# Merge gates in a stage of their own: twelve projection tiles as six Strassen pairs behind pa, attention left with q and k

## The chip, the cores and the metric

The kernel runs on one core of one Trainium2 chip. The metric is the time on the device in microseconds (us), the median of several runs. TensorE (PE) multiplies matrices, VectorE (DVE) and ScalarE (ACT) work elementwise, GpSimd (POOL) issues some of the DMAs and does a little elementwise work, SyncE (SP) issues the other DMAs.

## The reference

One layer of a hybrid encoder on 512 tokens of width 1024, in float32. It is given x, the weights and the gains:

```python
h = rms_norm(x, mix_norm_pre)
proj = h @ w_in                      # 1024 x 7696
xa, ga, q, k, v, f_logit, g_a, g_b = split(proj)
hr = rg_lru(causal_dwconv(xa), ...)  # recurrent branch, width 1280
y_a = gelu(ga) * hr
y_b = forgetting_attention(q, k, v, f_logit + b_forget)   # 16 heads of 64, causal
merged = (sigmoid(g_a + b_merge[0]) * (y_a @ w_proj_a)
          + sigmoid(g_b + b_merge[1]) * (y_b @ w_proj_b))
x = x + rms_norm(merged @ w_out, mix_norm_post)
h = rms_norm(x, ffn_norm_pre)
gate, val = split(causal_dwconv(h @ w_up))                # 1024 x 6144
x = x + rms_norm((gelu(gate) * val) @ w_down, ffn_norm_post)
```

In forgetting_attention the score of query i and key j is q·k/8 + cum[i] - cum[j], with cum the running sum of log_sigmoid(f). The change concerns g_a and g_b, each 1024 columns of w_in, and when they are computed.

## The kernel before

Each float32 operand is split into a high and a low part in a format that PE takes at full speed, and each product is made of three matmuls: high x high, high x low, low x high. `Split` does this for a weight tile: a load of 512 KB on SP's queue, the high part as a cast on ACT (`wh_...`, L172), the low part as a subtraction on DVE (`wl_...`, L175). A weight tile of w_in has 128 columns; `project` multiplies it with h (`hh`, `hl`, 1024 x 512 tokens) in 8 steps of three matmuls of 512 columns (L222 to L224), 24 in all. `order` lists the weight tiles in the order of their use, and `unit` fetches two ahead, so that list sets the order of the loads.

The stages follow one another on PE: xa and the recurrent gates, v (83 us), ga (136), pa (y_a @ w_proj_a, 190 to 248 us), attention with q, k and the gate tiles ma (to 426), then the tiles mb and pb (y_b @ w_proj_b), wo (517), up (562), dn (801).

The forget gate (`forget`, L626) is computed inside pa, after tile 4: 16 small matmuls, then a long chain of 16 x 512 operations on DVE (log-sigmoid, running sum), then four writes of cum to DRAM (`cnd`). A head's bias tile `B` is read back from there by a broadcast DMA, and two accumulating DMAs add the causal mask; both are issued by POOL (`prep_alloc`, L689). There are two such tiles per period.

Attention has eight periods of two heads. On PE a period is `ma`, `av` (probabilities x v of the heads before), scores, `q`, `k`, `pt` (transposes of the probabilities of this period's heads, which PE's next `av` wants). DVE adds the bias to the scores and takes the row's minimum (L726), ACT takes the exponential (L731), DVE divides by the sum (`normalise`, L738 and L741), then PE transposes in halves (L753), and ACT and DVE split the result (L763, L764). A gate tile's tanh is on ACT (L676), and ma is multiplied into `pa` on DVE (L802). The tiles mb0 to mb2 fill the end of attention, mb3 to mb7 stand between the tiles of pb.

The up stage (L927 to L930) already uses Strassen's form: a class `Pair` takes two weight tiles and computes both with seven products of half the size instead of eight. Each product is 12 matmuls of 256 columns (4 steps, three matmuls each). It needs sums of weight quarters (DVE, `sums`), their high and low parts, sums of quarters of h, and adds of the results. At two pairs (`TURNS`) eight small transposes stand before product 5. The low half of a plain quarter is made by ACT, with the sign turned, and a POOL-issued accumulating DMA (`ml`, L877).

Elsewhere a scheduler decides the place of an instruction within an engine from the order of the code and its waits; under `manual_schedule` the written order holds.

Of the kernel before, what the change touches and what calls it, by code (L numbers as in the profile page):

```python
# [8 lines left out]
F32 = mybir.dt.float32  # L9
# [7 lines left out]
P = 128  # L17
# [9 lines left out]
H = 16  # L27
# [36 lines left out]
def kernel(  # L64
# [120 lines left out]

    order = [(f"xa{t}", *cols(w_in, B_XA + t)) for t in range(TR)]
# [8 lines left out]
    for e in range(KD):  # L195
        if e >= 3:
            order.append((f"mb{e}", *cols(w_in, B_MB + e)))
        order.append((f"pb{e}", *cols(w_pb, e)))
# [110 lines left out]
    def v_out(c, pv):  # L309
        for t in range(NT):  # L310
            pvv = pv[t].rearrange("p (q j d) -> p q j d", q=4, j=2)
            for q in range(4):
                p = 4 * c + q
                vh = vt[p][:, t, 0:4:3, :]
                act.copy(vh, pvv[:, q])
                dve.tensor_tensor(out=vt[p][:, t, 1:3, :], in0=pvv[:, q], in1=vh.bitcast(F32), op=ALU.subtract)

    with ExitStack() as rg:
# [303 lines left out]
        papool = mstk.enter_context(tc.tile_pool(name="pa", bufs=1, reuse_waits="tile"))  # L622
        pa = papool.tile([P, KD, S], F32, name="pa")
        cnd = ctx.enter_context(tc.tile_pool(name="cnd", bufs=1, space=bass.MemoryType.DRAM)).tile([H, PO[NT]], F32, name="cnd")

        def forget():  # L626
            def tl(name, n=H, dt=F32):
                return tpool.tile([P, S], dt, tag="tt", name=f"f_{name}")[0:n]

            fr = tl("fr", P)[:, : KD * H].rearrange("p (k e) -> p k e", k=KD)  # L630
            nc.sync.dma_start(fr, w_f)
            fw = tl("fw", P, F32R)[:, : KD * 48].rearrange("p (k e) -> p k e", k=KD)
# [7 lines left out]
            z = tl("z")  # L640
            act.copy(z, pf[32:48])
            dve.scalar_tensor_tensor(out=z, in0=pf[0:H], scalar=cpt[0:H, C_BF : C_BF + 1], in1=z, op0=ALU.add, op1=ALU.add)
            with tc.issue_after(last_act[0].ins):
                l1p = log1p_exp_neg(z, tl)
            dve.tensor_scalar(out=z, in0=z, scalar1=0.0, scalar2=None, op0=ALU.min)
            dve.scalar_tensor_tensor(out=z, in0=l1p, scalar=-2.0, in1=z, op0=ALU.mult, op1=ALU.add)
            ones = tl("ones")
            pool.memset(ones, 1.0)
            cum = tl("cum")
            dve.tensor_tensor_scan(out=cum, data0=ones, data1=z, initial=0.0, op0=ALU.mult, op1=ALU.add)  # L650
            dve.tensor_scalar(out=cum, in0=cum, scalar1=-8.0, scalar2=None, op0=ALU.mult)
            for b in range(NT):
                nc.sync.dma_start(cnd[:, PO[b] : PO[b + 1]], cum[:, : PO[b + 1] - PO[b]])

        pps = {}
        for e, half in PA_ORDER:
            if half == 0:
                pps[e] = bank(f"pa{e}")
            wh, wl = unit(f"pa{e}_{half}")
# [18 lines left out]

    with ExitStack() as at:
# [88 lines left out]
        def av(p, pts):  # L768
# [14 lines left out]
            yb[p] = vpools[p == 0 or p > 4].tile([P, 2, S], F32R, tag="vy", name=f"yb{p}")  # L783
# [3 lines left out]
        prev = None  # L787
        for p in range(KD):
            bias = prep_alloc(p)
            pq, pk = bank(f"q{p}"), bank(f"k{p}")  # L790
            project(pq, unit(f"q{p}"), hh, hl)
            if prev is not None:
                normalise(prev)
            project(pk, unit(f"k{p}"), hh, hl)
            q = halves(pq, f"q{p}")
            if p == 0:
                apool.tile([P, 64], F32, name="offset_k", bufs=1)
            k = halves(pk, f"k{p}")
# [4 lines left out]
            if prev is not None:  # L803
                av(p - 1, pts)
            prev = scores(p, q, k, bias)
        tgs = [gate_tile(0, "mb")]
        normalise(prev)
        tgs.append(gate_tile(1, "mb"))
        pts = pt(KD - 1, prev)
        tgs.append(gate_tile(2, "mb"))  # L810
# [10 lines left out]
    for e in range(KD):  # L821
        if e >= 3:
            tgs.append(gate_tile(e, "mb"))
# [26 lines left out]
    KH, SH = KD // 2, S // 2  # L850
    TURNS = (NU + 2, NU + 7)

    def sub(out, a, b):
        dve.tensor_tensor(out=out, in0=a, in1=b, op=ALU.subtract)  # L854

    A, B = slice(0, 512), slice(512, 1024)
    X, Y = slice(0, SH), slice(SH, S)

    def quarter(a, b, s):
# [651 lines left out]
```

## The time and the profile before

| | us |
|---|---|
| median of 3 runs (lowest, highest) | 927.65 (926.85, 929.72) |
| the profiled execution | 925.8 |
| its span in the profile | 924.0 |
| PE busy | 913.7 (99%) |
| PE weight loads busy (beside PE) | 797.6 (86%) |
| DVE busy | 685.0 (74%) |
| ACT busy | 565.7 (61%) |
| POOL busy | 223.0 (24%) |

The span goes from the first to the last instruction. PE's granted clock is full throughout. Busy shares are averages over stages: in pa DMA is nearly full and DVE half empty, in the up stage DVE is nearly full. PE is the engine that nearly never waits, so the questions to the trace are what its matmuls take and what could make it wait.

### The profile page before, as it was taken

What the parts mean: (1) busy time and instruction counts of PE and PEld (TensorE: products, weight loads), DVE (VectorE), ACT (ScalarE), POOL (GpSimd) and SP (SyncE); (2) the same over time, 40 slices, a digit from 0 to 9 for tenths busy, and PEclk for the clock granted to TensorE, in tenths of its full rate; (3) what the DMA queues carried; (4) which work ended last, traced back from release to release, by engine and by line L of the source; (5) the groups of instructions that cost most, each with busy time, mean ns of one, the idle gap of its engine ahead of it and who ended that gap; (6) DMA issues with size and microseconds to landing.
All of it is one profiled execution on the core that took longest, in us unless ns stands there. A gap on an engine that the chain in (4) does not pass through costs nothing.

```text
span 924.0 us, 15014 instructions
## 1 busy us (share of the span) xinstructions
PE 913.7 (99%) x5598; PEld 797.6 (86%) x5598; DVE 685.0 (74%) x1127; ACT 565.7 (61%) x981; POOL 223.0 (24%) x235
## 2 busy tenths in 40 slices
PE   8999999999999999999999999999999999999997
PEld 7988888887888888888888889999999999988885
DVE  5966369532857777777544588999899999889897
ACT  7555495333345666666333376698778887667664
POOL 4134345444243232220111000022232323100000
PEclk9999999999999999999999999999999999999999
DMA  7667589989686656653232764188888888799764
GB/s 278 236 210 209 162 203 257 278 215 258 164 229 153 165 149 153 153 151 80 72 111 91 273 184 159 38 227 223 213 231 206 239 204 203 225 347 335 250 212 146
DMA packets 76218, 182.29 MB, mean 197 GB/s; under 512 B 7281, under 2 KB 35745, under 8 KB 75762
## 3 DMA queue, kind: packets, MB, share of 16 engines
q1 hardware_dynamic: 44912, 122.87, 39.7%
q0 software_dynamic: 30944, 57.94, 30.4%
q8 instruction: 44, 0.72, 0.3%
q10 hardware_dynamic: 290, 0.53, 0.1%
q14 instruction: 28, 0.23, 0.1%
HBM read 148.59 MB, written 33.64 MB: 197 GB/s over the span
## 4 chain that ended last, share of the span: by engine, by line
PE 96%; DVE 2%; ACT 1%; DMA 1%; issue 0%; SPq 0%; DVEq 0%; ACTq 0%
PE up L927 7%; PE up L930 7%; PE up L928 7%; PE dn L1234 4%; PE dn L1233 4%; PE dn L1232 4%; PE ga L223 2%; PE ga L222 2%; PE pa L224 2%; PE pa L222 2%; PE pa L223 2%; PE ga L224 2%; PE ma L222 2%; PE q L222 2%; PE wo L846 2%; PE mb L222 2%
## 5 line engine op out<-in xcount | busy, mean ns | idle before, releaser
L1085 DVE SCALAR_TENSOR_TENSOR u<-up,cpt,u 128x511 f32<-128x511 f32 x96 | 71.3, 746 | 2.6 <-ACT u L1079 0.9
L877 POOL DMA_DIRECT2D ml<-raw_up x41 | 35.1, 856 | 144.3 <-ACT mh L886 75.7
L1234 PE MATMUL dn<-wh_dn,al 128*128 128x512 f32 x168 | 65.6, 391 | 0.1
L1232 PE MATMUL dn<-wh_dn,ah 128*128 128x512 f32 x168 | 65.4, 389 | 0.0
L1233 PE MATMUL dn<-wl_dn,ah 128*128 128x512 f32 x168 | 65.4, 389 | 0.0
L927 PE MATMUL up<-sh,th 128*128 128x256 f32 x252 | 61.2, 279 | 0.7 <-ACT x L934 0.6
L928 PE MATMUL up<-sl,th 128*128 128x256 f32 x252 | 60.8, 277 | 0.0
L175 DVE TENSOR_TENSOR wl_dn<-raw_dn,wh_dn 128x1024 fp32r<-128x1024 f32 x42 | 51.5, 1227 | 8.7 <-ACT wh_dn L172 8.7
L172 ACT CAST wh_dn<-raw_dn 128x1024 fp32r<-128x1024 f32 x42 | 44.1, 1050 | 16.3 <-issue 6.0
L854 DVE TENSOR_TENSOR tl<-t,th 128x1024 fp32r<-128x1024 f32 x42 | 51.2, 1218 | 1.3 <-ACT th L908 1.3
L927 PEld LDWEIGHTS up<-sh,th 128*128 128x128 f32 x252 | 47.4, 188 | 1.2 <-ACT x L934 0.8
L928 PEld LDWEIGHTS up<-sl,th 128*128 128x128 f32 x252 | 47.4, 188 | 0.0
L696 POOL DMA_DIRECT2D B<-maskf x32 | 39.4, 1635 | 28.2 <-DMA B<-cnd 24.9
L908 ACT CAST th<-t 128x1024 fp32r<-128x1024 f32 x42 | 44.0, 1048 | 3.0 <-PE up L223 0.8
L1093 POOL TENSOR_TENSOR yf<-u,u 128x512 f32<-128x512 f32 x20 | 25.9, 1296 | 79.8 <-issue 66.8
L1079 ACT ACTIVATE u<-up,cpt 128x512 f32<-128x512 f32 x48 | 36.9, 775 | 12.3 <-POOL yf L1093 8.0
L927 PE MATMUL up<-h2h,mh 128*128 128x256 f32 x168 | 40.5, 277 | 0.0
L928 PE MATMUL up<-h2l,mh 128*128 128x256 f32 x168 | 40.5, 277 | 0.0
L930 PE MATMUL up<-sh,tl 128*128 128x256 f32 x252 | 39.1, 277 | 0.0
L1234 PEld LDWEIGHTS dn<-wh_dn,al 128*128 128x128 f32 x168 | 31.5, 188 | 7.4 <-DVE al L854 0.8
L934 ACT COPY x<-up 128x256 f32<-128x256 f32 x63 | 23.1, 367 | 23.7 <-PE up L930 23.6
L175 DVE TENSOR_TENSOR wl_pa<-raw_pa,wh_pa 128x640 fp32r<-128x640 f32 x16 | 13.1, 820 | 32.7 <-ACT wh_pa L172 32.7
(655 smaller groups left out, 3174.8 us busy)
## 6 DMA issues: line engine op xcount, KB each, us to landing
raw_up<-in_w_up_dram SPq DMA_DIRECT2D x48, 512.0 KB, 5.4
td<-in_w_down_dram POOLq DMA_DIRECT2D x36, 512.0 KB, 7.9
raw_dn<-td SPq DMA_DIRECT2D x24, 512.0 KB, 5.0
B<-cnd POOLq DMA_DIRECT2D x16, 640.0 KB, 5.0
ml<-raw_up POOLq DMA_DIRECT2D x20, 512.0 KB, 5.7
raw_dn<-in_w_down_dram SPq DMA_DIRECT2D x18, 512.0 KB, 4.3
raw_wo<-in_w_out_dram SPq DMA_DIRECT2D x16, 512.0 KB, 3.8
td<-td POOLq DMA_DIRECT2D x12, 512.0 KB, 10.7
```

Source lines behind the costliest of these rows:

```text
L172: act.copy(self.wh, self.raw)
L175: engine.tensor_tensor(out=self.wl, in0=self.raw, in1=self.wh.bitcast(F32), op=ALU.subtract)
L222: pe.matmul(dst, ah, bh, start=first, stop=False)
L854: dve.tensor_tensor(out=out, in0=a, in1=b, op=ALU.subtract)
L908: act.copy(self.th[i], self.t[i])
L927: pe.matmul(dst, wh[:, k], ah[:, k], start=first and k == 0, stop=False, skip_group_check=True)
L928: pe.matmul(dst, wh[:, k], al[:, k], start=False, stop=False, skip_group_check=True)
L930: pe.matmul(dst, wl[:, k], ah[:, k], start=False, stop=k == KH - 1, skip_group_check=True)
L1085: dve.scalar_tensor_tensor(out=c[:, s:], in0=ps[:, : S - s], scalar=col(C_CFW + 3 * e + j), in1=c[:, s:], op0=ALU.mult, op1=ALU.add)
L1232: pe.matmul(dst[t], ah[:, k, tok], wh[:, k], start=first, stop=False, skip_group_check=True)
L1233: pe.matmul(dst[t], ah[:, k, tok], wl[:, k], start=False, stop=False, skip_group_check=True)
L1234: pe.matmul(dst[t], al[:, k, tok], wh[:, k], start=False, stop=last, skip_group_check=True)
```

## The change

Six pairs (ma e, mb e), e = 2 to 7 (`M0` is 2), are computed by `Pair` in a stage of their own behind pa. ma0 and ma1 stay plain and stand at its start; mb0 and mb1 stay plain and stand at the end of attention. `Pair` is made general (a `Stage` holds its pools and operands) and moves up in the file. The gates mb2 to mb7 are written to DRAM (`mbd`) and read back during pb. The forget gate is computed before pa, between it and the end of ga. `h_sums` computes the sums of quarters of h, in the memory that later holds half of pa's results. The attention loop has the order av, k, normalise, pt, q, scores. `hh` and `hl` stay until mb1, and one buffer of the value pool moves to a pool of its own (`vy2`).

```diff
-    for p in range(KD):
-        order.append((f"q{p}", *cols(w_in, B_Q + p)))
-        order.append((f"k{p}", *cols(w_in, B_K + p)))
-        order.append((f"ma{p}", *cols(w_in, B_MA + p)))
-    order += [(f"mb{e}", *cols(w_in, B_MB + e)) for e in range(3)]
...
+    order += [(f"ma{e}", *cols(w_in, B_MA + e)) for e in range(M0)]
+    order += [proj("q", 0), proj("k", 0), proj("q", 1)]
+    for p in range(1, KD):
+        order.append(proj("k", p))
+        if p + 1 < KD:
+            order.append(proj("q", p + 1))
+    order += [(f"mb{e}", *cols(w_in, B_MB + e)) for e in range(M0)]
+    order += [(f"pb{e}", *cols(w_pb, e)) for e in range(KD)]
...
+        with tc.tile_pool(name="forget", bufs=1, reuse_waits="tile") as fpool:
+            forget(fpool)
...
+        def h_sums(i, sh=sh, sl=sl):
+            c1, c2 = (slice(P * (i + d), P * (i + 1 + d)) for d in (0, 2))
+            f = pa[:, KH:].rearrange("p a (k c) -> p a k c", k=KH)
+            f11, f12, f21, f22 = (f[:, a] for a in range(4))
+            for dst, k, c in ((f21, 0, c2), (f22, KH, c2), (f11, 0, c1), (f12, KH, c1)):
+                dve.tensor_tensor(out=dst, in0=hh[:, k : k + KH, c].bitcast(F32), in1=hl[:, k : k + KH, c].bitcast(F32),
+                                  op=ALU.add)
...
+            for n, src in enumerate((f22, f11, f21, f12)):
+                act.copy(sh[n][:, :, c1], src)
+                dve.tensor_tensor(out=sl[n][:, :, c1], in0=src, in1=sh[n][:, :, c1].bitcast(F32), op=ALU.subtract)
...
-            if (e, half) == (4, 1):
-                forget()
...
+            if (e, half) in ((2, 0), (1, 1)):
+                h_sums(half)
...
+        m_pair = lambda p: Pair(mstg, p, (w_in[B_MA + p], w_in[B_MB + p]))
+        gate_tile(0, "ma", 1)
+        mp = {M0: m_pair(M0)}
+        gate_tile(1, "ma", 0)
...
+        def m_out(b, which):
+            tg = gate_act(b.c if which == "mb" else b.a, b.j, which)
+            if which == "mb":
+                nc.sync.dma_start(mbd[b.j], tg)
+
+        def m_period(j):
+            p, b, n1, n2 = mp[j], mp.get(j - 1), mp[j + 1], mp[j + 2]
+            if b:
+                p.p5()
+                b.add(b.c[:, Y], b.a[:, Y], 1)
+                b.add(b.c[:, X], b.c[:, X], 0)
+            n1.plain(1)
+            if b:
+                m_out(b, "mb")
+                p.keep(1, p.c[:, X])
+                n1.sums(0)
+            p.product(6, p.a[:, Y])
...
+                b.product(4, b.a[:, Y])
+                m_out(b, "ma")
...
+            p.product(3, p.c[:, X])
+            n2.plain(0)
+            n1.p12()
...
+            m_load(j)
+            p.product(7, p.a[:, Y])
...
+        prev = scores(0, qs[0], ks[0], bias)
         for p in range(KD):
-            bias = prep_alloc(p)
-            pq, pk = bank(f"q{p}"), bank(f"k{p}")
-            project(pq, unit(f"q{p}"), hh, hl)
-            if prev is not None:
-                normalise(prev)
-            project(pk, unit(f"k{p}"), hh, hl)
...
-                pts = pt(p - 1, prev)
-            tg = gate_tile(p, "ma")
-            dve.scalar_tensor_tensor(out=pa[:, p], in0=tg, scalar=1.0, in1=pa[:, p], op0=ALU.add, op1=ALU.mult)
-            if prev is not None:
+            if p:
                 av(p - 1, pts)
-            prev = scores(p, q, k, bias)
-        tgs = [gate_tile(0, "mb")]
+            if p + 1 < KD:
+                bias = prep_alloc(p + 1)
+                ks[p + 1] = projected("k", p + 1)
+            else:
+                tgs.append(gate_tile(0, "mb"))
+            normalise(prev)
+            pts = pt(p, prev)
+            if p + 2 < KD:
+                qs[p + 2] = projected("q", p + 2)
+            if p + 1 < KD:
+                prev = scores(p + 1, qs[p + 1], ks[p + 1], bias)
...
     for e in range(KD):
-        if e >= 3:
-            tgs.append(gate_tile(e, "mb"))
+        if e + 1 >= M0 and e + 1 < KD:
+            tgs.append(tgps[-1].tile([P, S], F32, tag="tg", name=f"tg_mb{e + 1}"))
+            nc.sync.dma_start(tgs[-1], mbd[e + 1])
         pb = bank(f"pb{e}")
```

Two places show how the order on DVE moves. The first is pa. Before, DVE has there only the low parts of pa's weights (`wl_pa`), and from tile 6 on the chain of the forget gate (`f_...`):

```order
L175 TENSOR_TENSOR wl_pa5_0_2142<-raw_pa5_0_2140,wh_pa5_0_2141 128x640
L175 TENSOR_TENSOR wl_pa5_1_2165<-raw_pa5_1_2163,wh_pa5_1_2164 128x640
L175 TENSOR_TENSOR wl_pa6_0_2245<-raw_pa6_0_2243,wh_pa6_0_2244 128x640
L175 TENSOR_TENSOR wl_pa6_1_2268<-raw_pa6_1_2266,wh_pa6_1_2267 128x640
L642 SCALAR_TENSOR_TENSOR f_z_2210<-f_2193,cpt_82,f_z_2210 16x512
L268 SCALAR_TENSOR_TENSOR f_y_2213<-f_z_2210 16x512
L645 TENSOR_SCALAR f_z_2210<-f_z_2210 16x512
L271 TENSOR_SCALAR f_d_2216<-f_y_2213 16x512
L272 RECIPROCAL f_d_2216<-f_d_2216 16x512
```

After, in the same place of pa, the sums of h (`pa<-hh,hl` and `pa<-pa`, 128 x 512) and their low parts (`msl`) stand between the low parts of the weights:

```order
L175 TENSOR_TENSOR wl_pa5_0_2245<-raw_pa5_0_2243,wh_pa5_0_2244 128x640
L784 TENSOR_TENSOR pa_2005<-hh_117,hl_118 128x512 x4
L786 TENSOR_TENSOR pa_2005<-pa_2005 128x512
L175 TENSOR_TENSOR wl_pa5_1_2268<-raw_pa5_1_2266,wh_pa5_1_2267 128x640
L787 TENSOR_TENSOR pa_2005<-pa_2005 128x512
L792 TENSOR_TENSOR msl0_2013<-pa_2005,msh0_2012 128x4x128
L788 TENSOR_TENSOR pa_2005<-pa_2005 128x512
L792 TENSOR_TENSOR msl2_2017<-pa_2005,msh2_2016 128x4x128
L789 TENSOR_TENSOR pa_2005<-pa_2005 128x512
L792 TENSOR_TENSOR msl1_2015<-pa_2005,msh1_2014 128x4x128
```

The forget chain has gone ahead of these rows, and the low part of pa5_1 stands behind the first five sums.

The second place is an attention period. `P6`, `P7` are the probabilities of heads 6 and 7, `s6`, `s7` their scores, `B` the bias tiles, `y2` the sum of the two halves of `av`'s result of the heads before. Before, DVE adds y ahead of the bias steps:

```order
L782 TENSOR_TENSOR y2_3287<-av4_3289,ytmp2_3288 64x512
L782 TENSOR_TENSOR y2_3287<-av5_3300,ytmp2_3288 64x512
L726 ISA P6_3344,mx6_3345<-s6c_3316,B6_3099 128x512
L726 ISA mx6_3345 128x1
L726 ISA P7_3355,mx7_3356<-s7c_3319,B7_3103 128x512
L726 ISA mx7_3356 128x1
L785 TENSOR_TENSOR yb2_3311<-y2_3287,yb2_3311 128x512
L726 ISA P6_3344,mx6_3345<-s6b_3315,B6_3099 128x256
L726 ISA mx6_3345 128x1
L726 ISA P7_3355,mx7_3356<-s7b_3318,B7_3103 128x256
```

After, y is added between the steps of the second head's normalising:

```order
L981 RECIPROCAL sm6_4158<-sm6_4158 128x4
L984 TENSOR_SCALAR P6_4156<-P6_4156,sm6_4158 128x512
L984 TENSOR_SCALAR P6_4156<-P6_4156,sm6_4158 128x384
L984 TENSOR_SCALAR P6_4156<-P6_4156,sm6_4158 128x128
L984 TENSOR_SCALAR P6_4156<-P6_4156,sm6_4158 128x256
L981 RECIPROCAL sm7_4169<-sm7_4169 128x4
L984 TENSOR_SCALAR P7_4167<-P7_4167,sm7_4169 128x512
L1025 TENSOR_TENSOR y2_4178<-av4_4180,ytmp2_4179 64x512
L1025 TENSOR_TENSOR y2_4178<-av5_4191,ytmp2_4179 64x512
L984 TENSOR_SCALAR P7_4167<-P7_4167,sm7_4169 128x384
L984 TENSOR_SCALAR P7_4167<-P7_4167,sm7_4169 128x128
```

The adds of y have moved behind the bias steps and the first head's normalising, and three of the second head's four steps stand behind them.

## Rows read from the trace of the kernel before

**Rows 1.** The page, part 1: engine, busy us (share of the span), instructions.
```profile
PE 913.7 (99%) x5598; PEld 797.6 (86%) x5598; DVE 685.0 (74%) x1127; ACT 565.7 (61%) x981; POOL 223.0 (24%) x235
```

**Rows 2.** Waits of PE: waiting line, releaser, us in all, times, longest.
```profile
PE xa L421 <- POOL ident masks.py:199: 1.5, 1, 1.5
```

**Rows 3.** Windows: pa, one attention period, the Strassen part of the up stage.
```profile
core 0: us, PE busy (x) PEld busy (x) DVE busy (x) ACT busy (x) POOL busy (x), PEclk, DMA share, GB/s
190.00:248.00 58.00, 58.00 (x257) 46.94 (x256) 27.59 (x34) 19.76 (x28) 23.62 (x27) 1.00 0.96 215
324.67:347.36 22.69, 22.69 (x156) 19.06 (x152) 16.65 (x44) 13.83 (x35) 6.93 (x7) 1.00 0.56 149
597.30:800.60 203.30, 202.59 (x1771) 201.66 (x1770) 186.64 (x274) 163.00 (x252) 58.02 (x59) 1.00 0.85 219
```

**Rows 4.** Timeline of PE at three seams: start, us, engine, line, operation.
```profile
135.82 0.39 PE L222 MATMUL ga<-hh,wh_ga 128*128 128x512 f32 x1
...
190.22 0.39 PE L222 MATMUL pa<-yh,wh_pa 128*128 128x512 f32 x1
...
248.33 0.39 PE L222 MATMUL q<-hh,wh_q 128*128 128x512 f32 x1
```

**Rows 5.** Timeline of PE, 256-column matmuls of the up stage.
```profile
562.29 0.28 PE L222 MATMUL up<-h2h,wh_up 128*128 128x256 f32 x1
...
573.48 0.28 PE L224 MATMUL up<-h2h,wl_up 128*128 128x256 f32 x1
...
642.10 0.63 PE L930 MATMUL up<-sh,tl 128*128 128x256 f32 x4
...
643.51 0.64 PE L930 MATMUL up<-h2h,tl 128*128 128x256 f32 x4
...
669.51 0.46 PE L946 MATMUL up<-ident 64*128 64x64 f32 x8
...
672.30 0.62 PE L930 MATMUL up<-sh,tl 128*128 128x256 f32 x4
...
673.66 0.62 PE L930 MATMUL up<-h2h,tl 128*128 128x256 f32 x4
```

**Rows 6.** DMA issues: tile, queue, count, KB each, us to landing.
```profile
ml<-raw_up POOLq DMA_DIRECT2D x20, 512.0 KB, 5.7
...
B<-maskf POOLq DMA_DIRECT2D x32, 128.0 KB, 5.2
```

**Rows 7.** Timeline of DVE in pa (columns as in rows 4).
```profile
191.75 0.69 DVE L592 TENSOR_TENSOR gelu<-gelu,ix 128x512 f32<-128x512 f32 x1
...
228.73 0.74 DVE L642 SCALAR_TENSOR_TENSOR f_z<-f,cpt,f_z 16x512 f32<-16x512 f32 x1 [2.90 <-ACT f_z L641]
...
250.16 0.41 DVE L651 TENSOR_SCALAR f_cum<-f_cum 16x512 f32<-16x512 f32 x1
```

**Rows 8.** Timeline of PE, one attention period.
```profile
307.56 0.39 PE L777 MATMUL av<-PTh,v 128*128 128x512 f32 x1
...
310.13 0.49 PE L717 MATMUL s4c<-h_k,h_q 64*128 64x512 f32 x1
...
312.20 0.50 PE L222 MATMUL q<-hh,wh_q 128*128 128x512 f32 x1
...
323.29 0.71 PE L753 MATMUL pt<-ident,P 64*128 64x64 f32 x16
```

**Rows 9.** Timeline of DVE, the same period.
```profile
310.36 1.40 DVE L782 TENSOR_TENSOR y<-av,ytmp 64x512 f32<-64x512 f32 x2
311.80 0.69 DVE L726 CUSTOM_DVE_ANT_0 P<-s4c,B 128x512 f32<-128x512 f32 x1
...
317.81 1.27 DVE L741 TENSOR_SCALAR P<-P,sm 128x512 f32<-128x512 f32 x4
```

**Rows 10.** Timeline of POOL, the same period.
```profile
315.39 1.25 POOL L693 DMA_DIRECT2D B<-cnd  x2 [13.29 <-DVE mx L726]
...
323.24 2.42 POOL L696 DMA_DIRECT2D B<-maskf  x2 [0.49 <-DMA B<-cnd]
```

More of the change, by code (lines that the diff above doesn't have):

```diff
@@ L316, in v_out, with sub, quarter, __init__ @@
                 dve.tensor_tensor(out=vt[p][:, t, 1:3, :], in0=pvv[:, q], in1=vh.bitcast(F32), op=ALU.subtract)
+    KH, SH = KD // 2, S // 2
+    def sub(out, a, b):
+        dve.tensor_tensor(out=out, in0=a, in1=b, op=ALU.subtract)
+    A, B = slice(0, 512), slice(512, 1024)
+    X, Y = slice(0, SH), slice(SH, S)
+    def quarter(a, b, s):
+        return tuple(x[:, s].rearrange("p (k e) -> p k e", k=KH) for x in (a, b))
+    class Stage:
+        def __init__(self, name, turns=()):
+            self.name, self.turns = name, turns
@@ new lines @@
+        with tc.tile_pool(name="forget", bufs=1, reuse_waits="tile") as fpool:
+            forget(fpool)
+        papool = mstk.enter_context(tc.tile_pool(name="pa", bufs=1, reuse_waits="tile"))
+        pa = papool.tile([P, KD, S], F32, name="pa")
+        mstg = Stage("m")
+        sums = ExitStack()
+        spool = sums.enter_context(tc.tile_pool(name="msums", bufs=1, reuse_waits="tile"))
+        sh, sl = {}, {}
+        for pad, parts in ((0, (3,)), (192, (0, 1, 2))):
+            if pad:
+                spool.tile([P, pad // 4], F32, name="offset_ms")
+            for i in parts:
+                sh[i] = spool.tile([P, KH, SH], F32R, name=f"msh{i}")
+                sl[i] = spool.tile([P, KH, SH], F32R, name=f"msl{i}")
@@ L658 @@
                 pps[e] = bank(f"pa{e}")
-            wh, wl = unit(f"pa{e}_{half}")
+            wh, wl = unit(f"pa{e}_{half}", min(2, where["ma0"] - where[f"pa{e}_{half}"]))
             for i in range(5):
@@ new lines, with gate_act @@
+    mbd = [ctx.enter_context(tc.tile_pool(name=f"mbd{e}", bufs=1, space=bass.MemoryType.DRAM)).tile([P, S], F32, name=f"mbd{e}")
+           for e in range(KD)]
+    tgps = []
+    def gate_act(pg, e, which):
+        c = 0 if which == "ma" else KD
+        tg = tgps[-1].tile([P, S], F32, tag="tg", name=f"tg_{which}{e}")
+        act.activation(out=tg, in_=pg, func=AF.Tanh, scale=0.5, bias=hb[:, c + e : c + e + 1])
+        if which == "ma":
+            dve.scalar_tensor_tensor(out=pa[:, e], in0=tg, scalar=1.0, in1=pa[:, e], op0=ALU.add, op1=ALU.mult)
+        return tg
@@ L679 @@
+    sums.close()
+    vpools.append(mstk.enter_context(tc.tile_pool(name="vy2", bufs=1, reuse_waits="tile")))
+    tgps.append(mstk.enter_context(tc.tile_pool(name="tg", bufs=3, reuse_waits="tile")))
     with ExitStack() as at:
@@ L806, with projected @@
-        tgs = [gate_tile(0, "mb")]
-        normalise(prev)
+        def projected(n, p):
+            if (n, p) == ("q", 0):
+                ps = pq
+            else:
+                ps = bank(f"{n}{p}")
+                project(ps, unit(f"{n}{p}"), hh, hl)
+            return halves(ps, f"{n}{p}")
+        qs = {0: projected("q", 0)}
+        apool.tile([P, 64], F32, name="offset_k", bufs=1)
+        ks = {0: projected("k", 0)}
+        bias = prep_alloc(0)
+        qs[1] = projected("q", 1)
```

304 lines of the change are left out of this document (175 added, 129 removed).

## The prediction

> **What bounds the kernel now.** I read the page's first part before all else: TensorE (PE) is busy 913.7 of 924.0 us, VectorE (DVE) 685.0, ScalarE (ACT) 565.7, GpSimd (POOL) 223.0 [rows 1]. Then the waits of PE: the longest is 1.5 us, and it lies at the start [rows 2]. So PE never waits for long; a change is worth what it takes out of PE's stream of matmuls, less the new waits that it makes there. Hence the table of windows, stage by stage: it shows how much of DVE, ACT and DMA lies under PE where the change adds work and where it takes cover away [rows 3]. In pa (190 to 248) DVE is busy 27.59 of 58.00 us; one attention period takes 22.69 us of PE, beside 16.65 of DVE. Last, PE's timeline gives the price of one matmul in each width, and DVE's and POOL's the chain of one attention period.
>
> **What is removed.** Twelve tiles (ma and mb of e = 2 to 7) leave attention and pb, each 24 matmuls of 512 columns. From the first of ga at 135.82 to the first of pa at 190.22 stand 10 tiles, 240 matmuls, without a gap [rows 4]: 54.40 / 240 = 0.2267 us each. 288 x 0.2267 = 65.3 us.
>
> **What is added.** Six pairs, each of 7 products of 12 matmuls of 256 columns: 42 products. The kernel already has such products in its up stage, and they run at two speeds: the groups at 642.10 and 643.51 stand one product apart, 1.41 us; those at 672.30 and 673.66 stand 1.36 apart [rows 5]. The speed changes at the little transposes (669.51), not at a wait, and the first 256-column matmuls after a 512-column stage (562.29 to 573.48, 95 spacings) took 11.19 / 95 = 0.1178 us each, 1.41 a product, until the next transposes [rows 5]. So 42 x 1.36 = 57.1 or 42 x 1.41 = 59.2. The new stage also follows 512-column work, which speaks for the slow speed, but which of the two a stage inherits I can't read from one entry; the whole up stage, 147 products in 203.30 us with its waits [rows 3], stands at 1.38. I take 1.385, between both: 58.2. Exchange: -7.1 us (ends -8.2 and -6.1).
>
> At full speed 256 columns cost half of 512 (1.36 / 12 = 0.1133 against 0.2267) [rows 4, 5], so the width costs nothing there; at the slow speed it costs 4%. The Trainium skill, Perfetto Trace Analysis, section Optimizing Tensor Performance, says that larger matmuls are more efficient than smaller ones, which speaks against this form; by it alone all 42 products run slow and the exchange would be -6.1, the time 923.7. The trace bears it out in one part of the up stage and not in the other.
>
> **Does the new stage feed PE?** One pair per 9.5 to 9.9 us needs on DVE two sum steps, two low parts and the adds (about as in up, where DVE is busy 186.64 of 203.30 us for 21 pairs and with conv and GeLU beside them [rows 3]); here conv and GeLU are absent. PE ran in up nearly without a gap, so I add nothing per pair. The seam is the start: the first pair's low half comes by an accumulating transfer of 5.7 us [rows 6]. Its ACT part can start when pa ends (248.3 [rows 4]); two plain tiles, ma0 and ma1, cover 2 x 5.44 = 10.9 us; by my walk through the order the transfer lands some 2.6 us before the first product wants it. I allow 0.3 to 0.4 us for small bubbles (0 to 3).
>
> **pa gets DVE work.** The half-sums of h are 24 more operations on 128 x 512 (the multiply of that size at 191.75 took 0.69 us [rows 7]) and 8 casts on ACT: DVE goes from 27.6 to about 44 of 58 us. They write into the memory that later holds pa, and the chain of the forget gate, which ran on DVE from 228.73 to 250.16 [rows 7], now stands before pa. Its 16 small matmuls only move. Beginning in ga's tail it ends by my walk at about 216, its four writes have landed near 219.5, and the sums follow in the order that DVE shows, with the low parts of pa5_1 to pa7_1 between them. The tightest is the low part of pa6_1: ready about 236, wanted at 238. Cost 0; if the sums come 2 us later than I think, each us shows on PE (0 to 3).
>
> **Attention loses its cover.** Before, one period is ma, av, scores, q, k, pt on PE: av 2.57 us (307.56 to 310.13), scores 2.07 (310.13 to 312.20), then q and k, and pt from 323.29, 1.4 [rows 8]. From the start of the scores to pt lie 13.2 us, and the normalising on DVE, second head from 317.81, four of 1.27 us in all, was done at 319.0 [rows 9]: 4.3 us early. After, a period is scores, av, k, pt, q. Its PE time is 22.69 - 5.44 = 17.25 us, and from scores to pt only 2.07 + 2.57 + 5.44 = 10.1 us remain, plus 0.75 for the first head's transposes before the second head is wanted. The chain beside it, from the end of q: the low half of q on DVE comes first (wl_q must pass as well), so the first bias step starts 2.8 us later than PE's q ends, where before it started 1.67 after the scores did (311.80 against 310.13 [rows 8, 9]). The bias steps and exponentials end at 8.0, the first head's normalising 1.4 us later, and the second head's four are split by the two adds of y (1.40 together [rows 9]), which now wait for av: it ends at 10.7 to 11.0, wanted at 11.05. Slack falls from 4.3 us to about nothing. I take 0.1 us per period for seven periods, 0.7 (0 to 2.5). In the first period no av stands between scores and pt, and 2.57 us of cover are missing, of which k's place gives part back: 1.1 us once (0.8 to 1.5).
>
> **Moved transfers.** The six mb gates go out (256 KB each) and come back on SP's queue during pb, where the row before had weights only; x2t (2 MB) is issued there once mb1 is done. I find nothing late behind them, since pb's weights stand ahead of them in the queue: 0 (0 to 1).
>
> **Sum.** -65.3 + 58.2 + 0.4 + 0.7 + 1.1 = -4.9 us. The profiled execution took 925.8 us (span 924.0 and 1.8 around it) and gives 920.9; the median of the runs shown is 927.65, 1.85 above it, and gives **922.7 us**.
>
> **Rivals.**
> 1. The bias tiles bind (slower). A head's bias tile is refilled when its last bias step has read it. In the trace the refill starts at 315.39, its masks are issued until 323.24 plus 2.42 [rows 10], and a mask takes 5.2 to land [rows 6]: I read 14.2 us from release to the last landing. The first step of the next period needs the last mask, and the steps of a head take 2.65 us more: a loop of 16.8 us against a period of 17.25. Before, 22.69 left over 5 us of room; now 0.4. One bias landing or mask landing that is 2 us later in the denser stretch makes 18.8, so 1.55 us in each of 6 to 7 periods, +10: about 932.5. It decides from a loop of 18.0 on: there 0.75 x 6.5 = 4.9 eats the gain. For it: the slack is small, and mask landings differ by more than this. Against it: DMA is busy 0.56 of the period [rows 3], with room left, and POOL loses no time to other work there. The skill's DMA: Bandwidth & Descriptors, section Latency and other measured facts, gives 0.2 us for an HBM access on average and 2 us at high load; two such steps in a row would add an estimated 3.6 us to the loop. No run here shows it.
> 2. The slow speed everywhere. If the new transposes and stages leave the up stage in the slow speed all through, its products from 669.51 to 800, about 96 of 147, cost 0.05 more each, +4.9, and the new ones +1.0: 922.7 + 5.9 = 928.6, no gain. For it: the speed changed at each of the transposes seen, and so depends on what came before. Against it: nothing between wo and the end is reordered.
> 3. The whole exchange is kept: all products at 1.36 and no stall in attention: 925.8 - 8.2 + 0.4 = 918.0, on the median 919.9.
> 4. Small losses add up: pa's low parts 2 us late, or the attention chain 0.6 us late in seven periods (4.2): 925 to 927.
>
> **Chances.** Forecast (920.5 to 924.6) 0.52; rival 3 0.10; rival 4 0.16; rival 2 0.08; rival 1 0.14. A measurement of this kernel tells 0.3%, 2.8 us, from no change. Faster (below 924.9): forecast, rival 3 and a little of 4, 0.64. Same: the rest of 4, rival 2 and a mild rival 1, 0.23. Slower: 0.13. The range leaves out most of rival 1 and the edge of rival 3: 919.3 to 927.8.
>
> **What would show it.** PE between the end of pa and q1: 42 products, 57 to 59 us, no wait over 1 us. The attention period on PE 17.25 to 17.5, its wait, if any, of pt on DVE's normalising; if the scores' readers wait for a mask instead, rival 1 is on. One wait of about 1 us at the first pt. PE's waits in pa none. In up the products from the second turn at 1.36. I am wrong if the attention period exceeds 18, or if the up stage differs from 203.3 by over 2 us.

## The result and the profile after

The changed kernel is slower: 932.0 us in the median (928.31 to 935.76, 20 runs) against 928.03 of the kernel before; ratio 1.0041, 95% interval 1.003 to 1.0052. The forecast was 922.7, a gain. Its profiled execution has a span of 927.7 us, 3.7 more than the one of before.

The page of the changed kernel, part 1 (busy us, share, instructions) and the row of the granted clock in 40 slices:

```profile
PE 915.2 (99%) x5814; PEld 806.6 (87%) x5814; DVE 724.3 (78%) x1193; ACT 592.8 (64%) x1031; POOL 242.5 (26%) x247
...
PEclk9999999999999999999899999999999999999999
```

The first row answers to [rows 1]. The exchange took matmul work away, yet PE is busy 915.2 us, 1.5 more than before. And one digit of the clock is an 8, where the row of before had only 9s. What the clock costs is hidden in PE's busy time, so the list of waits doesn't show it. That list, for PE of the changed kernel (waiting line, releaser, us in all, times, longest):

```profile
PE xa L531 <- POOL ident masks.py:199: 1.5, 1, 1.5
PE s15c L960 <- DVE l_k L947: 1.2, 1, 1.2
...
PE pt L996 <- DVE P L984: 0.4, 1, 0.4
```

There is one new wait over 1 us, at s15c, the scores of head 15. From starts on PE's timelines of the two kernels, stage by stage:

| stretch | before, us | after, us |
|---|---|---|
| up to ga | 135.82 | 136.41 |
| ga and pa (with the forget gate's matmuls) | 112.51 | 112.51 |
| end of pa to wo | 268.67 | 270.59 |
| of it: ma0, ma1 and the 42 products (the last one stands behind q0) | | 10.88 + 58.77 |
| of it: attention with mb0, mb1; pb | | 157.34; 43.60 |
| wo and up | 283.59 | 284.08 |
| dn to the end | 123.4 | 124.1 |

The loss is in attention. Its 18 tiles take 18 x 5.44 us and the rest of eight periods 51.0 (before: 268.67 less 40 tiles), together 148.9; it took 157.34, 8.4 more. The next view shows where. It is the table of windows of the changed kernel, for pa, the products up to q0, one attention period, and then the last period in steps of 4 us:

```profile
core 0: us, PE busy (x) PEld busy (x) DVE busy (x) ACT busy (x) POOL busy (x), PEclk, DMA share, GB/s
190.80:248.90 58.10, 58.10 (x257) 47.06 (x256) 42.77 (x61) 23.30 (x35) 32.27 (x24) 1.00 0.82 187
259.80:317.10 57.30, 57.30 (x493) 57.22 (x492) 33.70 (x49) 36.48 (x58) 7.96 (x10) 1.00 0.75 184
385.80:403.20 17.40, 17.40 (x131) 14.47 (x130) 15.19 (x41) 11.98 (x32) 6.06 (x6) 1.00 0.70 169
448.00:452.00 4.00, 2.78 (x44) 1.84 (x42) 3.94 (x8) 3.72 (x9) 3.85 (x4) 1.00 0.80 167
452.00:456.00 4.00, 3.75 (x23) 3.08 (x23) 3.82 (x11) 1.22 (x5) 0.98 (x1) 0.74 1.06 188
456.00:460.00 4.00, 4.00 (x14) 3.49 (x14) 3.87 (x19) 3.97 (x15) 0.00 (x0) 0.50 0.07 9
460.00:464.00 4.00, 4.00 (x20) 3.47 (x19) 3.67 (x10) 2.25 (x6) 0.00 (x0) 0.90 0.00 0
```

The first three windows are as they should be (they answer to [rows 3]): no idle PE in pa, though DVE went from 27.59 to 42.77 us; none among the products; a period of 17.40. The last four are not. From 448 to 456 PE is idle 1.47 us in all, and from 452 to 464 the clock is at 0.74, 0.50 and 0.90. 0.50 is the lower of its two levels, 1.2 GHz. PE's timeline of this place, answering to [rows 8]:

```profile
450.38 0.50 PE L960 MATMUL s14c<-h_k,h_q 64*128 64x512 f32 x1
452.09 0.49 PE L960 MATMUL s15c<-h_k,h_q 64*128 64x512 f32 x1 [1.21 <-DVE l_k L947]
...
454.37 0.55 PE L960 MATMUL s14b<-h_k,h_q 64*128 64x256 f32 x1 [0.16 <-DVE PTl L1007]
...
456.19 0.79 PE L1020 MATMUL av<-PTh,v 128*128 128x512 f32 x1
...
460.87 0.44 PE L223 MATMUL mb<-hh,wh_mb 128*128 128x512 f32 x1
```

From 450.38 to 456.19 lie the scores, 5.81 us where they took 2.07 before; from 456.19 to 460.87 av, 4.68 where it took 2.57. That is 5.8 us in one period. It has three parts. PE is idle for 1.5 us. The low clock takes about 3.2 (an estimate: 0.26 of 4 us in the window from 452, and the 2.1 by which av is longer). About 1.2 are left, and they belong to the scores themselves: before, the matmuls of two heads start in pairs (s4c and s5c both at 310.13) and run side by side, while here s14c starts 1.71 us ahead of s15c, and for stretches one head's matmuls run alone. What the scores waited for is on DVE's timeline, answering to [rows 9]:

```profile
448.28 1.30 DVE L984 TENSOR_SCALAR P<-P,sm 128x384 f32<-128x384 f32 x3
449.50 0.67 DVE L1028 TENSOR_TENSOR yb<-y,yb 128x512 fp32r<-128x512 f32 x1
450.10 1.21 DVE L175 TENSOR_TENSOR wl_pb<-raw_pb,wh_pb 128x1024 fp32r<-128x1024 f32 x1
451.34 0.69 DVE L947 TENSOR_TENSOR l_k<-k,h_k 128x512 fp32r<-128x512 f32 x1
451.95 1.28 DVE L1007 TENSOR_TENSOR PTl<-pt,PTh 128x512 fp32r<-128x512 f32 x2
...
454.74 0.48 DVE L1007 TENSOR_TENSOR PTl<-pt_r,PTh 128x128 fp32r<-128x128 f32 x2
```

The low half of the last k (`l_k`) is written at 451.34, behind the rest of the normalising, the low part of yb and the low part of a weight of pb (`wl_pb`). Behind `l_k` come the low parts of the probabilities (`PTl`), until 455.2. The scores need `l_k`, and they need six banks of PSUM (the memory that PE writes its results to), which the transposes before them fill and which are free once DVE has read them for `PTl`. In every other period q's projection stands between pt and the scores, 5.44 us of cover for all this. There is no ninth q.

### The profile page after: what moved, and what is told of

Read it like the earlier page. It is cut to its first block, busy times and chain, and to the rows that moved or that the text cites. A ratio compares the mean times of both kernels' runs of the same rounds, so it can differ in the third digit from the quotient of the medians.

```text
span 927.7 us, 15629 instructions
## 1 busy us (share of the span) xinstructions
PE 915.2 (99%) x5814; PEld 806.6 (87%) x5814; DVE 724.3 (78%) x1193; ACT 592.8 (64%) x1031; POOL 242.5 (26%) x247
## 4 chain that ended last, share of the span: by engine, by line
PE 90%; DVE 2%; DMA 2%; issue 2%; ACT 2%; SPq 0%; POOL 0%; DVEq 0%; POOLq 0%; ACTq 0%
PE a_up L406 5%; PE a_up L403 5%; PE a_up L404 5%; PE dn L1382 4%; PE dn L1380 4%; PE dn L1381 4%; PE pa L223 2%; PE pa L225 2%; PE ga L224 2%; PE ga L223 2%; PE pa L224 2%; PE ga L225 2%; PE c_up L403 2%; PE c_up L404 2%; PE c_up L406 2%
## 5 line engine op out<-in xcount | busy, mean ns | idle before, releaser
L360 POOL DMA_DIRECT2D ml_up<-raw_up x41 | 35.1, 856 | 146.6 <-ACT mh_up L369 75.7
L322 DVE TENSOR_TENSOR tl_up<-t_up,th_up 128x1024 fp32r<-128x1024 f32 x42 | 51.1, 1218 | 1.3 <-ACT th_up L391 1.3
L391 ACT CAST th_up<-t_up 128x1024 fp32r<-128x1024 f32 x42 | 44.0, 1047 | 3.8 <-DVE t_up L322 0.9
L974 ACT ACTIVATE P<-P,mx 128x512 f32<-128x512 f32 (+2 forms) x64 | 35.1, 550 | 16.0 <-DVE mx L969 16.0
L403 PE MATMUL a_up<-sh,th_up 128*128 128x256 f32 x168 | 40.7, 279 | 0.7 <-ACT x L410 0.6
L404 PE MATMUL a_up<-sl,th_up 128*128 128x256 f32 x168 | 40.5, 277 | 0.0
L403 PE MATMUL a_up<-h2h,mh_up 128*128 128x256 f32 x168 | 40.5, 277 | 0.0
L404 PE MATMUL a_up<-h2l,mh_up 128*128 128x256 f32 x168 | 40.5, 277 | 0.0
L359 ACT ACTIVATE ml_up<-raw_up 128x512 fp32r<-128x512 f32 (+1 forms) x41 | 34.3, 837 | 1.6 <-DMA raw_up<-in_w_up_dram 1.6
L369 ACT CAST mh_up<-raw_up 128x1024 fp32r<-128x1024 f32 (+1 forms) x42 | 34.9, 831 | 0.0
## 6 DMA issues: line engine op xcount, KB each, us to landing
td<-td POOLq DMA_DIRECT2D x12, 512.0 KB, 10.1
```

The lines of the kernel that those rows point to most:

```text
L391: act.copy(self.th[i], self.t[i])
L403: pe.matmul(dst, wh[:, k], ah[:, k], start=first and k == 0, stop=False, skip_group_check=True)
L404: pe.matmul(dst, wh[:, k], al[:, k], start=False, stop=False, skip_group_check=True)
```

## The experiments

Each ran beside the kernel before, in four groups (again to e3; e2_again to e6; e7, e4_again and before_no_turns; e8 and e7_again). The medians of before in them were 927.27, 926.47, 926.34 and 926.67, so between groups only the ratios compare. Medians and ratios to before, with the intervals:

| kernel | median, us | ratio |
|---|---|---|
| again (the changed kernel) | 930.29 | 1.0027 (1.001 to 1.0045) |
| e1_fill12 | 929.53 | 1.0025 (1.0003 to 1.0046) |
| e2_mb0_gap | 925.13 | 0.9967 (0.9947 to 0.9986) |
| e3_three_plain | 928.93 | 1.0017 (1.0002 to 1.0032) |
| e2_again | 925.56 | 0.9991 (0.9972 to 1.001) |
| e4_no_turns | 922.36 | 0.9962 (0.9942 to 0.9982) |
| e6_lk_early | 929.44 | 1.0026 (1.0009 to 1.0043) |
| e7_dve_low | 921.72 | 0.9963 (0.9943 to 0.9982) |
| e4_again | 924.34 | 0.9977 (0.9959 to 0.9995) |
| before_no_turns | 929.83 | 1.0024 (1.0006 to 1.0041) |
| e8_both | 924.37 | 0.9974 (0.9955 to 0.9993) |
| e7_again | 923.74 | 0.9966 (0.9942 to 0.999) |

**The end of attention.** First the changed kernel as it is:

> The changed kernel once more, beside the kernel before on the same chip. Both theories: 1.004 of before, granted clock 0.995, and PE from the scores of heads 14 and 15 (s14c) to the first matmul of pb about 25.5 us where its work alone is 19.7.

It kept the wait (1.3 us at s15c) and the low clock (0.65 from 452 to 456); s14c to pb took 23.38 us, in the first profile 25.53. So the place is the same, and its price differs between executions: 25.5 us were expected. Then matmuls without use in the place of the missing q:

```diff
+            elif p + 2 == KD:
+                fill = bank("fill")
+                for k in range(4):
+                    mm3(fill, lastw[0][0][:, k], lastw[0][1][:, k], hh[:, k], hl[:, k], k == 0, k == 3)
```

> Twelve matmuls of 512 columns (2.72 us, result unused) stand on PE between the last transposes of heads 12, 13 and the scores of heads 14, 15, where each other period has a q. Theory A (the missing q lets PE wait for the low half of k7, PE's granted clock then falls to half, the two together 5.8 us): no wait at s15c, clock 1.00 in all windows, s14c to pb 19.7 to 20.2 us, the whole 5.8 - 2.7 = 3.1 us faster than the changed kernel, ratio to before 1.000 to 1.002. Rival B (the denser attention is short of DVE or DMA time, the wait is only where it shows): the wait moves on, the time is that of the changed kernel plus 0 to 2.7. Rival C (the clock falls for another reason than this wait): wait gone, 1.2 to 1.7 us won and 2.7 paid, low clock stays, ratio 1.005.

The windows of e1_fill12 at the same place (columns as above):

```profile
452.00:456.00 4.00, 4.00 (x36) 3.35 (x35) 3.71 (x11) 1.98 (x4) 1.16 (x1) 1.00 0.68 77
456.00:460.00 4.00, 4.00 (x22) 3.42 (x22) 3.08 (x18) 3.98 (x17) 0.00 (x0) 1.00 0.31 122
```

PE is busy all through, the clock is 1.00, and s14c to pb took 20.17 us. The scores of the two heads run in pairs again, as on PE's timeline of e1_fill12:

```profile
452.51 0.49 PE L960 MATMUL s14c<-h_k,h_q 64*128 64x512 f32 x1
452.51 0.49 PE L960 MATMUL s15c<-h_k,h_q 64*128 64x512 f32 x1
```

In this stretch theory A holds and rival C falls: the low clock goes with the wait. From ga to wo the profile of e1 took 379.44 us, 3.7 and 2.6 less than the two of the changed kernel (383.10 and 382.00), where 3.1 were expected. The median doesn't show it (929.53 against 930.29, with overlapping intervals); the two speeds of the up stage, below, lie over it. The next one adds no work, only order:

```diff
             else:
-                tgs.append(gate_tile(0, "mb"))
+                tgs.append(gate_tile(1, "mb"))
             normalise(prev)
...
+            elif p + 2 == KD:
+                tgs.append(gate_tile(0, "mb"))
...
-        tgs.append(gate_tile(1, "mb"))
+        pb0, pw0 = bank("pb0"), unit("pb0")
+        for k in range(KD - 1):
+            mm3(pb0, pw0[0][:, k], pw0[1][:, k], yb[k][:, 0], yb[k][:, 1], k == 0, False)
         av(KD - 1, pts)
```

> Only the order: mb0 takes q's place in the last period, mb1 the place of k, and the first seven steps of pb0 stand between the last transposes and the last av. No work added. Theory A: clock 1.00, the time 5.8 us less than the changed kernel (up to 0.5 back at the last av, whose cover is 4.8 us for a chain of 4.8), ratio to before 0.998. Rival B: no more than 1.5 us won, ratio 1.0025 or more. Rival C: 1.5 us won, low clock stays.

The median is 5.2 us less than that of the changed kernel beside it, the ratio is 0.9967, and no window is under 0.99 of the clock from 440 to 480 us. In the profiles, ga to wo took 378.49 us, 4.6 and 3.5 less than in the two of the changed kernel. This is near theory A's 5.8, and rival B, that the denser attention is short of DVE or DMA, is out: its periods are as dense as in the changed kernel. e3 does the same with one pair less (mb2 stands where e2 has the first part of pb0):

```diff
-    M0 = 2
+    M0 = 3
...
         gate_tile(0, "ma", 1)
+        gate_tile(1, "ma", 1)
         mp = {M0: m_pair(M0)}
-        gate_tile(1, "ma", 0)
+        gate_tile(2, "ma", 0)
```

> One pair less (five; ma2 and mb2 plain), mb0 in q's place of the last period, mb1 in k's, mb2 behind the last transposes. A pair costs 9.76 us in the new stage against 10.88 as two plain tiles, so +1.1 us. Theory A: 5.8 - 1.1 = 4.7 us less than the changed kernel, ratio to before 0.999. Rival B: 1.0025 or more. Rival C: low clock stays, 1.004.

In its profile PE has no new wait, and ga to wo takes 378.81 us, 4.3 less than in the changed kernel (383.10) where 4.7 were expected; but the median is only 1.4 less. Eleven of its twelve times lie between 927.87 and 931.58; its profiled execution had the slow up stage. The median is a miss. Last, DVE's order alone, with a fetch made to come after `l_k`:

```diff
+                if n == "pb1":
+                    late.enter_context(tc.issue_after(special["lk"].ins))
                 w = Split(src, shape, n, special.get(n))
```

> The changed kernel with one instruction moved: the low part of pb1's weight stands behind the low half of k7 on DVE, not ahead of it, so l_k7 and the steps behind it come 1.15 us earlier; PE's order is unchanged. If the wait for l_k7 by itself does the harm: the 1.2 us at s15c are gone, the clock stays up, 4 to 5 us are won, ratio to before 0.999. If the scores also wait for the six banks that the transposes hold until DVE has read them (the last of PTl, about 454): waits of 1 us or more stay spread over the scores, the clock still falls, and 1 to 2 us are won, ratio 1.002 to 1.003.

Three small waits of PE remain, on its timeline of e6_lk_early:

```profile
451.44 0.50 PE L963 MATMUL s14c<-h_k,h_q 64*128 64x512 f32 x1
452.17 0.50 PE L963 MATMUL s15c<-h_k,h_q 64*128 64x512 f32 x1 [0.23 <-DVE l_k L950]
...
453.36 0.44 PE L963 MATMUL s15a<-h_k,h_q 64*128 64x384 f32 x1 [0.16 <-DVE PTl L1010]
...
454.45 0.35 PE L963 MATMUL s14b<-h_k,h_q 64*128 64x256 f32 x1 [0.30 <-DVE PTl L1010]
...
455.05 0.35 PE L963 MATMUL s15b<-h_k,h_q 64*128 64x256 f32 x1
```

The wait for `l_k` fell from 1.21 to 0.23 us, and the waits for the banks (`PTl`) stay, as the second case said, though they are 0.16 and 0.30 us and not 1. s14c to pb took 22.23 us, 1.2 to 3.3 less than in the two profiles of the changed kernel, but 2.1 more than in e1. In the profiled execution the clock stayed at 1.00, against the second case. With the clock full the scores still took 4.41 us (451.44 to 455.85) in place of 2.07, and PE was idle for only some 0.8 of the 2.3 lost: the rest goes with the heads being out of step (s14c 0.73 ahead of s15c, s14b 0.60 ahead of s15b). Its profile also lost 1.8 us at the start of the new stage (below). Over the timed executions the mean clock reads 0.992 to 0.999, so in some it probably fell; the ratio of 1.0026 shows no gain over the changed kernel's 1.0027. Advancing one operand wasn't enough.

**The start of the new stage.** e2 once more, beside the next two:

> The kernel of e2_mb0_gap once more, beside the next two. 0.9967 of before again (0.995 to 0.9985), no window under 0.99 of the clock between 440 and 480 us. Theory D (the speed of the 256-column products is set anew in each execution, not by the program): its up stage takes either about 238.5 or about 242.5 us, whichever this execution drew.

Its ratio was 0.9991 (in e2 0.9967), outside the expected range, and its median 925.56 (in e2 925.13). The end of attention kept its full clock. The up stage took 238.76 us from the first up matmul to dn, where the profile of e2 had 243.39: one program, two times, as theory D said (more on it below). The profile shows another wait, which the changed kernel's first profile had not (again: 1.2 us). PE's timeline of e2_again, at the first pair's product 1:

```profile
263.79 1.23 PE L406 MATMUL a_m<-hh,ml_m 128*128 128x256 f32 x4 [2.08 <-DMA ml_m<-raw_m]
264.81 0.41 PE L403 MATMUL a_m<-hh,mh_m 128*128 128x256 f32 x1
```

The windows of e2_again around it:

```profile
256.00:260.00 4.00, 4.00 (x20) 3.30 (x19) 3.50 (x6) 2.75 (x4) 1.72 (x2) 1.00 1.06 151
260.00:264.00 4.00, 1.93 (x13) 1.61 (x12) 0.69 (x1) 0.69 (x1) 0.00 (x0) 0.96 1.10 212
264.00:268.00 4.00, 4.00 (x23) 4.00 (x24) 0.13 (x1) 0.54 (x2) 0.00 (x0) 0.61 1.01 293
```

PE waits 2.08 us for the accumulating transfer of the first low half, and from 264 to 268 the clock is at 0.61. From the first ma to q0 this execution took 71.86 us, the changed kernel's first profile 68.22. POOL's timeline of e2_again tells one reason why the transfer is late:

```profile
252.95 1.01 POOL L130 DMA_DIRECT2D td<-td  x1 [8.96 <-DMA td<-td]
253.58 0.58 POOL L149 COPY tick<-wh_pa 128x1 f32<-128x1 f32 x1
253.70 1.30 POOL L360 DMA_DIRECT2D ml_m<-raw_m  x1
```

ACT had made its part of `ml_m` by 251.5. But POOL issues in order, and ahead of the transfer stand a background transfer of the dn weights (`td`), which itself waited for another `td` until 252.95, and the small copy behind it. The transfer was issued at 253.70, 2.2 us behind ACT's part, and landed 10.1 us later. In the eight profiles with this start (after, again, e1, e2, e2_again, e4, e6, e4_again) the wait was 0, 1.2, 0, 0.8, 2.1, 1.8, 1.8 and 1.1 us. A low clock followed it in two of them (e2_again and e4), not in e6. The late issue is much the same in seven of the eight, 2.2 to 2.6 us behind ACT's part (0.8 in e1), with a wait or without. What differs is the landing: 7.9 us after the issue in the first profile, 8.3 in e1, 8.8 to 10.1 in the six that waited, where the transfers of this kind in [rows 6] took 5.7. In windows of 2 us from 250 to 262 the DMA share reads 1.08 to 1.20 in the first profile and 0.87 to 1.21 in e2_again, so DMA was close to full without a wait as well as with one. Why one transfer lands later than another stays open. The repair was tried on a kernel without the sixteen transposes, which is e4, below:

```diff
-            p.plain_lo(0)
             p.sums_hi(0)
-            p.plain(0)
+            p.plain(0, True)
             p.sums_lo(0)
```

> e4 with the low half of the first pair's first tile made by DVE (1.2 us) in place of ACT and the accumulating transfer. Theory F (that transfer is issued on POOL behind a background transfer that waits for another one, lands late in some executions, PE waits 0 to 2.1 us for it and its clock falls for some us behind it): no wait of PE at a_m, clock 1.00 from 248 to 300 us, the stretch from the first ma to q0 68.0 to 68.3 us where e4 took 71.7 and the changed kernel 68.2; on the median 1.5 to 2 us less than e4. Rival G (the transfers of the next pairs are as late): PE waits at c_m or the next a_m instead, the stretch stays over 69.

No wait of PE in the new stage, 68.04 us from the first ma to q0, no low clock: so the wait was for this transfer, as theory F has it, and rival G fell. The repair takes the late issue and the slow landing away together, so the share of each isn't shown. The median is 2.6 under e4_again beside it and 0.6 under e4; the intervals overlap, so the wait's end is shown and its worth in the median is not. Repeated:

> e7_dve_low once more: ratio to before 0.996 (0.994 to 0.998), two groups of times some 6 us apart, no wait at the first product 1.

It came out as expected: 0.9966, no such wait, 68.04 us from the first ma to q0, and times from 918.26 to 921.59 (six) and 925.89 to 928.55 (six).

**The two speeds of the 256-column products.** The changed kernel's first profile and its repetition, one program, run the up stage differently. PE's timeline of the first, at two places (the last four matmuls of neighbouring products):

```profile
642.26 0.63 PE L406 MATMUL a_up<-sh,tl_up 128*128 128x256 f32 x4
...
643.68 0.64 PE L406 MATMUL c_up<-sh,tl_up 128*128 128x256 f32 x4
...
691.61 0.62 PE L406 MATMUL a_up<-sh,tl_up 128*128 128x256 f32 x4
...
692.97 0.62 PE L406 MATMUL c_up<-sh,tl_up 128*128 128x256 f32 x4
```

and of the repetition:

```profile
641.49 0.62 PE L406 MATMUL c_up<-sh,tl_up 128*128 128x256 f32 x4
...
642.85 0.62 PE L406 MATMUL a_up<-sh,tl_up 128*128 128x256 f32 x4
...
691.88 0.63 PE L406 MATMUL a_up<-sh,tl_up 128*128 128x256 f32 x4
...
693.29 0.63 PE L406 MATMUL a_up<-h2h,tl_up 128*128 128x256 f32 x4
```

The first takes 1.42 and then 1.36, the repetition 1.36 and then 1.41: the same program drew the opposite speed, and so its up stage took 242.06 us from the first up matmul to dn instead of 238.78. Without the transposes that turn it:

```diff
-    up = Stage("up", (NU + 2, NU + 7))
+    up = Stage("up")
```

> e2 without the sixteen small transposes at two pairs of the up stage. Theory D: the products after the start of the up stage stay at one speed to its end, and which one differs from execution to execution: times in two groups some 6 to 7 us apart (130 products x 0.054), the lower near 920, the upper near 927, and the median anywhere between. Rival E (the speed belongs to the place in the program and the transposes set it): one group, with a spread as in e2, at 1.2 us less for the transposes and 35 x 0.054 = 1.9 less or 5.1 more for the speed.

Eight times lie from 918.66 to 923.24 and four from 926.23 to 927.84; in the profiled execution (922.65) all 132 products behind the start take 1.36. This is theory D, against rival E. Again:

> e4_no_turns once more, beside e7: 0.996 of before, times in two groups. Theory F: a wait of 0 to 2.1 us at the first product 1 of the new stage, and the low clock behind it only where the wait is near 2.

Here the median was 924.34 and the two groups are less clear (920.59 to 930.18). The wait at product 1 was 1.1 us, and no low clock followed. Next, the kernel before without its transposes:

```diff
-    TURNS = (NU + 2, NU + 7)
+    TURNS = ()
```

> The kernel before without the sixteen small transposes. It tells how much of e4's gain is theirs. If the speed is drawn in each execution with even chances, the median stays that of before less 0 to 2 us, in two groups some 6 us apart; if most executions draw the fast one (as two thirds did in e4), 2 to 3 us less than before, ratio 0.997 to 0.998, and e4's gain over it is 1 to 3 us.

Three times lie from 923.94 to 926.06 and nine from 929.42 to 932.04; the profiled execution (930.26) is a slow one, 129 products at 1.41. The median of 929.83 is a miss, since neither case had it above before's. Of the five profiles without transposes the one with fast products (e4) lies in the lower group of times, and those with slow ones (e4_again, e7, e7_again and this one, 928.07 to 930.26) lie high. So without its transposes the kernel before draws too, and its slower median goes with the draw; leaving out the transposes is by itself no gain here. The shares of the draw differ between the kernels (3 of 12 fast here, 8 of 12 in e4). What decides it stays open, and so does whether some of the 0.4% is a worse draw.

**Both repairs.**

> The changed kernel with both repairs and the transposes of the up stage kept: mb0, mb1 and the first part of pb0 moved as in e2, the first low half on DVE as in e7. If the end of attention and the start of the new stage are what the forecast missed, the time is near the one that was forecast: 922.5 to 924.5, ratio to before 0.995 to 0.998; the stretch from the first ma to q0 is 68.0 to 68.3 us, the first s14c to the rest of pb0 about 19.4 us, the clock 1.00 in both. If something else was missed too, the ratio stays at e2's 0.9967 to 0.9991 or above.

The windows of e8_both, the new stage with its two plain tiles and then the last period:

```profile
248.30:316.40 68.10, 68.10 (x542) 66.19 (x541) 42.88 (x61) 43.62 (x67) 10.90 (x14) 1.00 0.77 182
449.00:456.00 7.00, 7.00 (x44) 5.66 (x44) 5.40 (x11) 4.37 (x10) 3.16 (x3) 1.00 0.90 150
456.00:460.00 4.00, 4.00 (x31) 3.58 (x28) 3.75 (x17) 2.90 (x9) 0.00 (x0) 1.00 0.39 131
```

Clock 1.00, no idle PE, 68.04 us from the first ma to q0, 19.41 from s14c to the rest of pb0. Its profiled execution drew the same speeds in the up stage as the profile of before, so the two can be set against each other: 922.0 against 925.8, 3.8 us less. From ga to wo it took 376.63 us against 381.18, 4.6 less. Median and ratio (0.9974, 0.9955 to 0.9993) are in the expected range. Of the variants with both repairs e7 has the lowest ratios, 0.9963 and 0.9966, and both intervals lie below 1; but the intervals of e2, e4 and e8 overlap them, so which of these is the fastest isn't shown.

## Why the prediction was wrong

**The exchange: nearly right.** -7.1 forecast; 42 products took 58.77 us, so -6.5. The reading behind the speed was wrong. In the new stage it changes within each pair; PE's timeline, one row per product (7, 5, 6, 4, 3):

```profile
280.48 0.62 PE L406 MATMUL a_m<-msh,tl_m 128*128 128x256 f32 x4
...
281.84 0.62 PE L406 MATMUL c_m<-msh,tl_m 128*128 128x256 f32 x4
...
283.20 0.62 PE L406 MATMUL a_m<-msh,tl_m 128*128 128x256 f32 x4
...
284.59 0.64 PE L406 MATMUL a_m<-hh,tl_m 128*128 128x256 f32 x4
...
286.01 0.63 PE L406 MATMUL c_m<-msh,ml_m 128*128 128x256 f32 x4
```

In pairs 3 to 7 products 5 and 6 take 1.36, product 4 1.39 (that of pair 7, behind q0, 1.43), the others 1.40 to 1.42, without a transpose between; in pair 2 products 5 and 6 take 1.40 and 1.41. By the rule on larger matmuls that the prediction cites from the Trainium skill (Perfetto Trace Analysis, section Optimizing Tensor Performance), the exchange would have been -6.1; the trace puts it between the two ends.

**pa, the bias tiles, the moved transfers: right.** No wait of PE in pa; the steps that read the bias tiles never waited for one, so rival 1 stayed off; the transfers on SP cost nothing that shows in PE's waits.

**The periods with a q: right.** 17.47 us in the mean from s2c to s12c (350.94 to 438.29, five periods) against 17.25 of work; 0.1 was forecast for each, it was 0.2. The first pt waited as said, in the forecast size:

```profile
344.30 0.91 PE L996 MATMUL pt<-ident,P 64*128 64x64 f32 x16 [0.44 <-DVE P L984]
```

From pt's start at 342.82 to q at 345.26 it took 2.44 us, 1.06 more than in [rows 3, 8] (323.29 to 324.67), and it began 0.2 later behind k than there: 1.25, forecast 1.1.

**The step that failed** is "After, a period is scores, av, k, pt, q", counted for seven periods alike. The order holds only while there is a q. The price of the last period, 5.8 us in the profile (3.7 in the repetition), was in no term, no rival and no bound. The walk that found slack at pt should have gone on to what the scores need: `l_k`, written behind all that DVE had put off, and the six banks. The second part of the price wasn't in my working at all: idle time of 1.5 us was followed by a clock of 0.50, and that cost more than the waits (about 3.2 us); about 1.2 more went because the two heads' scores no longer ran in pairs. The Trainium skill, Perfetto Trace Analysis, section Matmul Optimizations, says that the matmul engine scales its power with utilization and that matmuls should run back to back; this case's trace agrees, with 0.50 from 456 to 460 us behind a PE busy 2.78 and 3.75 of 4 us.

**The second step that failed** is "the transfer lands some 2.6 us before the first product wants it". The walk left out what stood ahead of the transfer on POOL's queue (2.2 us behind ACT's part in the first profile), and it took 5.7 us for the landing, from the up stage, where it was 7.9 to 10.1 here. Its cost, 0 to 2.1 us, and up to 3.6 with the clock, lies near the bound that was given (0 to 3). That the first profile shows 0 is luck: there the transfer landed just as the product wanted it.

**The sum as it was:** -6.5 for the exchange, +5.8 (or 3.7) at the last period, +2.6 in the other periods (8.4 - 5.8), 0 to 3.6 at the start of the stage. In the first profile that is -6.5 + 5.8 + 2.6 = +1.9; the other 1.8 of its 3.7 are 0.6 ahead of ga, 0.5 in wo and up and 0.7 in dn, small differences that I did not test. The medians differ by 4.0. With both repairs and the same speeds in the up stage the difference was -3.8, near the -4.9 that was forecast without these two prices. What the other periods lost beyond the 1.8 that was forecast for them, 0.8, was not looked into. **Rival 2** had the mechanism half right: the speed of the up stage does change, but from execution to execution (its Strassen part took 203.8 us in the first profile and 207.0 in the repetition, where it was 203.3 before), and without the transposes in both kernels.

## What to carry to other kernels

When a loop is rewritten so that one step covers another, walk the first and the last pass on their own: here the pass without the covering step was the one that paid. On an engine at 99%, price a new wait by what the clock does behind it as well, and look for it in the windows, since busy time hides it. Take the landing of a transfer from a stretch where DMA is as full as where it will stand. Before trusting a difference of 0.3%, look whether one program gives the same stage times twice.

## What was not expected of the hardware

Waits of 1.5 us spread over 8 us (448 to 456) were followed by the lower clock for some 7 us (0.74, 0.50 and 0.90 over 4 us each are 2.1, 4.0 and 0.8 us at 0.50), while a single wait of 1.8 us was followed by it in one execution and not in another. A product of twelve matmuls of 256 columns runs at 1.36 or 1.41 us, and which of the two holds in the up stage is drawn in each execution. With the transposes, behind which the speed turns, the stage took 238.8 or 242.1 us in two executions of the changed kernel; without them 235.5 (e4) or 242.6 (e4_again). What draws it stays open.
